# A convolution summed in PSUM, and a gate's tanh written where it is used

## The chip, the cores and the metric

The kernel runs on one core of one Trainium2 chip. The metric is the device time of one launch in microseconds, from runs on the chip: less is better. TensorE is called PE below, VectorE DVE, ScalarE ACT, GpSimd POOL, and SyncE, which only issues DMAs, SP.

## The reference

One inference step of a two-layer trunk: an RG-LRU layer (Hawk), then an HGRN2 layer, on 1024 prompt tokens and 8 sequences of 4 decode tokens, all in float32. The change concerns the first layer alone:

```python
xn = _rmsnorm(x, g_norm)
u = xn @ w_in                              # 1024 -> 2 * 1536
xb, gate = u[..., :W_LRU], u[..., W_LRU:]
xp = concatenate([buf, xb], axis=1)        # the causal convolution, 4 taps
xc = b + sum(w[k] * xp[:, k:k + T] for k in range(4))
xh = xc.reshape(Bsz, T, 16, 96)            # 16 blocks of 96 columns
r = sigmoid(einsum('btni,nij->btnj', xh, w_r) + b_r)
ig = sigmoid(einsum('btni,nij->btnj', xh, w_i) + b_i)
log_a = -8 * softplus(-lam) * r
a = exp(log_a)
bterm = sqrt(-expm1(2 * log_a)) * (ig * xc)
h = scan(a, bterm)                         # h[t] = a[t] * h[t-1] + bterm[t]
y = h * silu(gate)
x = x + y @ w_out
```

## The kernel before

All 1056 tokens lie along the free dimension in three chunks of 352 columns (the last chunk is 320 prompt columns and the 32 decode tokens); features lie on the 128 partitions. A product of two float32 matrices is made of three fp32r matmuls of rounded high and low parts (`mm3`, lines 290 to 292). Weights come in by DMA as `wraw`; ACT rounds them to the high part (`whi`, L436), and POOL or DVE subtracts to get the low part (`wlo`, L374).

PSUM has eight banks: four with the tag `mm`, taken in turn by the main products, and four with the tag `hg`, for the block-diagonal gate products and norms. A main product with 1024 inputs is 24 matmuls of 352 columns, an out product (`out`, a third of 1536 inputs) is 9.

The 1536 columns of the recurrent branch are worked on in four groups g = 0 to 3 of three 128-row tiles (j = 0 to 2). For each group there are gate products (`gate(g)`), conv products (`conv(g)`, nine of them: three tiles, three chunks), the recurrence (`lru(g)`) and the out products (`out(g)`). The main products follow each other in this order: the three chunks of gate(0) and conv(0), gate(1), conv(1), gate(2) with lru(1) beside it, conv(2), out(0) with lru(2) beside it, gate(3) for one tile, conv(3), out(1) with lru(3) beside it, the rest of gate(3), and the last out products (`out_last`).

*A conv product* ends in a `mm` bank `ps`. ACT copies it to `xb` (L578, in SBUF, with room for the three columns before it; in the first group DVE writes `xb` with the norm multiplied in), and the last three columns to the next `xb` (L581). In the third chunk POOL and ACT also build the windows of the decode tokens in `xb`, and every step is done once for 320 prompt and once for 32 decode columns. ACT writes tap 3 times its weight plus the bias to an SBUF row `t` (L591; `t` is one of three rows of the tile `k`). DVE adds the other three taps to `t` (L594), ACT rounds `t` to the high part in `Z` (L597), and DVE writes the low part (L598). The bank is free as soon as ACT has copied it out.

*The recurrence.* A group has 384 rows, which is four of the reference's blocks of 96. The fourth block is made of rows 32j to 32j + 31 of tile j; the other 96 rows of each tile are a block of their own. These are gathered by DMA into `fo` (six copies a chunk) and multiplied on their own. The tanh of the three plain blocks goes from an `hg` bank to `R` (L666, 128 rows). The fourth block's goes from its bank to `td`, a part of the tile `ST` (L672, 96 rows), and three DMAs copy its 32-row pieces into their places in `R`, over rows that L666 wrote. Then follow, for each tile, exp (L679) and tanh (L681) on ACT, the sum of the high and low part on POOL (L685, to one of two rows of `k`), DVE's L686, a square root on ACT (L689), two products on DVE (L690, L692), and the scan (L706) and the gate (L716).

*The order* on every engine is written out by a planner in the kernel, `Flow`. Each step is added with its engine, a cost in microseconds, the keys that it reads and writes (a bank or a row is a key), and a priority. `plan` lays all steps out in time, `back` gives them due times, and after some turns the best plan is emitted; each engine then runs its steps in exactly that order. For the first layer, a DMA is taken to land 2.6 us after its issue begins, and its bytes are added at 250 KB a microsecond. A DVE step with `both` is taken to wait for POOL's running step. The second layer has a plan of its own, which starts from the first one's end times.

Of the kernel before, what the change touches and what calls it, by code (L numbers as in the profile page):

```python
# [14 lines left out]
F32 = mybir.dt.float32  # L15
# [3 lines left out]
AF = mybir.ActivationFunctionType  # L19
ALU = mybir.AluOpType  # L20
# [30 lines left out]
CH = 352  # L51
# [9 lines left out]
class Flow:  # L61
# [67 lines left out]
    def plan(self, key, stop=None):  # L129

        n = len(self.ops)
        left = [len(o[3]) for o in self.ops]
        ready = list(self.born)
        wait = {e: [] for e in self.ENGINES}
        free = dict(self.busy)
        dma = locked = taken = 0.0
        for i in range(n):
            if not left[i]:
                wait[self.ops[i][0]].append(i)
        starts, ends, took, order = [0.0] * n, [0.0] * n, [0.0] * n, []  # L140
        for _ in range(n):
            t0, e = min((max(free[e], min(ready[i] for i in q)), e) for e, q in wait.items() if q)
            q = wait[e]
            i = min((j for j in q if ready[j] <= t0), key=lambda j: (key[j], j))
            q.remove(i)
            order.append(i)
            _, us, _, _, _, kb, _, both = self.ops[i]
            if both and not self.exact and free["POOL"] > t0:
                us = max(us, free["POOL"] - t0 + us - 0.13)
            elif both and self.exact:  # L150
                us += max(0.0, taken - t0 - 0.07)
                locked = t0 + us
            elif e == "POOL" and self.exact:
                us += max(0.0, locked - t0 - 0.035)
                taken = t0 + us
            starts[i] = t0
            free[e] = end = t0 + us
            if kb and self.exact:
                dma = max(dma + kb / 250.0, t0 + 2.4 + kb / 600.0)
                end = dma - 2.15 - kb / 250.0  # L160
            elif kb:
                dma = max(dma, t0 + 2.6) + kb / 250.0
                end = dma - 2.15 - kb / 250.0
            ends[i] = max(free[e], dma if kb else 0.0)
            took[i] = us
            if i == stop:
                break
            for j in self.after[i]:
                ready[j] = max(ready[j], free[e] if (i, j) in self.soft else end + self.lag(i, j))
                left[j] -= 1  # L170
                if not left[j]:
                    wait[self.ops[j][0]].append(j)
        last = max(t for t, o in zip(ends, self.ops) if self.until in (None, o[0]))
        return last, starts, ends, order, took
# [83 lines left out]
def tile_trunk(ctx: ExitStack, tc: tile.TileContext, xT, xN, prm, hc, w0, wg, wo0, w1, wo1, s_in,  # L258
               yT, h_out, c_out, sp_out, ss_out):
    nc = tc.nc  # L260
    V, S, G, T, Q = nc.vector, nc.scalar, nc.gpsimd, nc.tensor, nc.sync
# [16 lines left out]
    def pc(name, j, n=1):  # L278
        a = PRM[name][0] + j
        return P[:, a:a + n]  # L280
# [64 lines left out]
    with ExitStack() as l0:  # L345
# [16 lines left out]
        def act(n, emit, r, w, prio=5, more=0.0, chain=None):  # L362
            fl.add("ACT", (0.09 + 0.00088 * n if fl.exact else 0.25 + 0.0007 * n) + more, emit, r, w, prio, line=chain)
# [193 lines left out]
        def conv(g, head=False):  # L557

            items = []
            for j in range(3):  # L560
                m = 3 * g + j
                mine = {}

                def evac(c, ps, pk, by=None, j=j, m=m, mine=mine):
                    n = CH if c < 2 else 1024 - 2 * CH
                    if c == 0:
                        mine[0] = next(xbs)
                        pool(3, lambda xb=mine[0][0]: G.memset(xb[:, :3], 0.0), (), (mine[0][1],), 2)
                    elif head:
                        mine[c] = next(xbs)  # L570
                        pool(3, lambda xb=mine[c][0]: G.tensor_copy(xb[:, :3], tails[:, 4 * j:4 * j + 3]), (("tail", j),), (mine[c][1],), 0)
                    xb, xk = mine[c]
                    t, tk = next(ts)
                    if by:
                        dve(n, lambda: V.tensor_tensor(xb[:, 3:3 + n], ps[:, :n], by[0], op=ALU.mult), (pk, by[1]), (xk,), 0)
                        pool(3, lambda: G.tensor_copy(tails[:, 4 * j:4 * j + 3], xb[:, n:n + 3]), (xk,), (("tail", j),), 1)
                    else:
                        act(n, lambda: S.copy(xb[:, 3:3 + n], ps[:, :n]), (pk,), (xk,), 0)  # L578
                    if c < 2 and not by:
                        nx, nk = mine[c + 1] = (tails[:, 4 * j:], ("tail", j)) if head else next(xbs)  # L580
                        act(3, lambda: S.copy(nx[:, :3], ps[:, CH - 3:CH]), (pk,), (nk,), 0)  # L581
                    parts = [(xb[:, :3 + n], t[:, :n], lambda ap, i: ap[:, i:i + n], n)]
                    if c == 2:
                        xs = xb[:, 323:379].rearrange("p (b j) -> p b j", j=7)
                        pool(24, lambda: G.tensor_copy(xs[:, :, :3], cs[:, m]), (("hct",),), (xk,), 1)
                        act(32, lambda: S.copy(xs[:, :, 3:], ps[:, n:CH].rearrange("p (b j) -> p b j", j=4)), (pk,), (xk,), 0)
                        pool(3, lambda: G.tensor_copy(cst[:, m, 0, :], xb[:, 320:323]), (xk,), (("cst", m),), 4)
                        pool(24, lambda: G.tensor_copy(cst[:, m, 1:, :], xs[:, :, 4:7]), (xk,), (("cst", m, 1),), 4)
                        parts.append((xs, t[:, n:].rearrange("p (b j) -> p b j", j=4), lambda ap, i: ap[:, :, i:i + 4], 32))
                    for src, dst, sh, u in parts:  # L590
                        act(u, lambda src=src, dst=dst, sh=sh: S.activation(dst, sh(src, 3), AF.Identity, bias=pc("cb", m),  # L591
                                                                         scale=pc("cw", 36 + m)), (xk, ("P",)), (tk,), 1, 0.1)
                        for k in range(3):
                            dve(u, lambda src=src, dst=dst, sh=sh, k=k: V.scalar_tensor_tensor(  # L594
                                dst, sh(src, k), pc("cw", 12 * k + m), dst, op0=ALU.mult, op1=ALU.add), (xk, tk), (tk,), 1, True)
                    (a, ak), (b, bk) = xpart(j, 0, c), xpart(j, 1, c)
                    act(CH, lambda: S.copy(a, t), (tk,), (ak,), 1)  # L597
                    dve(CH, lambda: V.tensor_tensor(b, t, a.bitcast(F32), op=ALU.subtract), (tk, ak), (bk,), 1, True)  # L598

                items.append((w0[m], evac))  # L600
            return items

# [27 lines left out]
        def lru(g):  # L630
            for i, n in ((0, 4), (4, 2)):
                raw, rk = next(raws)
                u = 128 * n
# [13 lines left out]
            for c in range(NCH):  # L647
# [10 lines left out]
                for i, hb in ((0, hbr), (1, hbi)):  # L658
                    for j in range(3):
                        m = 3 * g + j  # L660
                        ps, pk = next(hg)
                        (a, ak), (b, bk) = xpart(j, 0, c), xpart(j, 1, c)
                        u = 3 * i + j
                        fl.add("PE", 0.48, lambda ps=ps, a=a, b=b, u=u: mm3(ps[:, :CH], (gh[:, u, :], gl[:, u, :]), a, b, True, True),
                               (ak, bk, ("gh", u // 4 * 4), ("gl", u // 4 * 4)), (pk,), 0)
                        act(CH, lambda ps=ps, R=R, i=i, j=j, hb=hb, m=m: S.activation(R[:, i, j], ps[:, :CH], AF.Tanh, bias=hb[:, m:m + 1],  # L666
                                                                           scale=0.5), (pk, ("sm",)), (("R", s, i, j),), 2, 0.05)
                    ps, pk = next(hg)

                    fl.add("PE", 0.48, lambda ps=ps, i=i: mm3(ps[:, :CH], (gsh[:, i, :], gsl[:, i, :]), fo[:, 0], fo[:, 1], True, True),  # L670
                           (("gs",), ("gsl",), ("fo",), *(("fo", n, j) for n in range(2) for j in range(3))), (pk,), 0)
                    act(CH, lambda ps=ps, i=i: S.activation(td[:, i], ps[:96, :CH], AF.Tanh, bias=hbd[:96, 4 * i + g:4 * i + g + 1],  # L672
                                                            scale=0.5), (pk, ("sm",)), [("ST", j, i) for j in range(3)], 2, 0.05)
                    for j in range(3):
                        w = slice(32 * j, 32 * j + 32)
                        dma(R[w, i, j], td[w, i], (("ST", j, i),), (("R", s, i, j),), 2, 45)
# [1363 lines left out]
```

## Time and profile before

| | |
|---|---|
| median of three runs | 1031.67 us (1030.27 to 1032.05) |
| the profiled execution | 1029.75 us |
| its span, first to last instruction | 1027.9 us |
| mean granted TensorE clock | 0.999 |
| busy: PE, DVE, ACT, POOL | 1013.2, 777.6, 610.3, 494.6 us |

The profile is of one execution. PE is its matmuls, PEld the weight loads that run beside them. A row of a group of instructions gives line, engine, operation, what is written and read (by the program's names, with shapes), how often, busy time, the mean in ns, and the idle time of that engine just before, with what ended it. "DVE R L686 <- DMA R<-ST" reads: DVE's instruction at line 686, which writes R, waited for the DMA that copies ST into R. Almost all DMAs of the first layer are issued from one line, L359, in SP's queue.

### The profile page before, as it was taken

How to read it: one execution, taken by the hardware profiler on the slowest of the kernel's cores; microseconds unless marked ns; L12 is line 12 of the kernel's file. 1: busy time of each engine (PE TensorE's matmuls, PEld its weight loads, DVE VectorE, ACT ScalarE, POOL GpSimd, SP SyncE). 2: the span in 40 equal slices, each digit the busy share in tenths (PEclk: the TensorE clock that was granted, in tenths of full speed). 3: DMA queues.
4: the chain of work that ended last, by engine and by line, in shares of the span. 5: the costliest groups of instructions: out<-in, count | busy, mean ns of one | idle time of the engine just before them, and what ended most of it. 6: DMA issues, size and time to landing. Idle time of an engine off the chain costs nothing.

```text
span 1027.9 us, 25651 instructions
## 1 busy us (share of the span) xinstructions
PE 1013.2 (99%) x9981; PEld 993.5 (97%) x9981; DVE 777.6 (76%) x1538; ACT 610.3 (59%) x1405; POOL 494.6 (48%) x579
## 2 busy tenths in 40 slices
PE   9999999999999999999999999999999999999997
PEld 9999999999999999999999999999999999999986
DVE  6899986798689688557798787787777777885537
ACT  7678656876765666434566474646565564752324
POOL 2435453454247254744235655564646464641544
PEclk9999999999999999999999999999999999999999
DMA  9611111214652478622113142423333333666204
GB/s 283 204 53 43 51 61 61 79 55 134 202 186 71 145 224 270 201 72 77 62 32 125 46 141 89 127 87 126 106 119 111 106 125 98 212 197 208 87 1 170
DMA packets 84442, 124.60 MB, mean 121 GB/s; under 512 B 11296, under 2 KB 61728, under 8 KB 84320
## 3 DMA queue, kind: packets, MB, share of 16 engines
q1 hardware_dynamic: 75104, 107.13, 33.6%
q10 hardware_dynamic: 9216, 15.84, 4.8%
q8 instruction: 78, 1.28, 0.5%
q14 instruction: 44, 0.36, 0.1%
HBM read 82.55 MB, written 33.87 MB: 113 GB/s over the span
## 4 chain that ended last, share of the span: by engine, by line
PE 86%; DVE 5%; ACT 3%; issue 2%; DMA 2%; POOL 1%; SPq 0%; POOLq 0%; DVEq 0%; ACTq 0%
PE mm L290 24%; PE mm L292 24%; PE mm L291 24%; PE hg L1281 2%; DVE k L594 2%; DMA R<-ST 1%; PE hg L1470 1%; PE hg L291 1%; PE hg L290 1%; PE hg L1513 1%; PE hg L292 1%; PE hg L1515 1%; PE hg L902 1%; PE hg L1538 1%; DVE R L706 1%
## 5 line engine op out<-in xcount | busy, mean ns | idle before, releaser
L290 PE MATMUL mm<-xh,whi 128*128 128x352 f32 (+1 forms) x1111 | 343.0, 309 | 0.3 <-DVE xo L737 0.3
L291 PE MATMUL mm<-xl,whi 128*128 128x352 f32 (+1 forms) x1111 | 340.8, 307 | 1.0 <-POOL xl L374 1.0
L292 PE MATMUL mm<-xh,wlo 128*128 128x352 f32 (+1 forms) x1111 | 341.5, 307 | 0.0
L374 POOL TENSOR_TENSOR wlo<-wraw,whi 128x256 fp32r<-128x256 f32 (+3 forms) x190 | 194.4, 1040 | 180.4 <-ACT whi L436 81.4
L291 PEld LDWEIGHTS mm<-xl,whi 128*128 128x128 f32 x1111 | 209.1, 188 | 1.5 <-POOL xl L374 1.2
L290 PEld LDWEIGHTS mm<-xh,whi 128*128 128x128 f32 x1111 | 208.8, 188 | 1.1 <-issue 0.6
L292 PEld LDWEIGHTS mm<-xh,wlo 128*128 128x128 f32 x1111 | 208.8, 188 | 0.2 <-DVE wlo L374 0.2
L290 PE MATMUL mm<-Z,whi 128*128 128x264 f32 (+1 forms) x507 | 152.2, 300 | 0.0
L291 PE MATMUL mm<-Z,whi 128*128 128x264 f32 (+1 forms) x507 | 150.5, 297 | 0.0
L292 PE MATMUL mm<-Z,wlo 128*128 128x264 f32 (+1 forms) x507 | 150.5, 297 | 0.0
L290 PEld LDWEIGHTS mm<-Z,whi 128*128 128x128 f32 x507 | 95.3, 188 | 2.7 <-ACT xh L1798 1.5
L594 DVE SCALAR_TENSOR_TENSOR k<-xb,prm_sb,k 128x352 f32<-128x352 f32 (+2 forms) x144 | 91.8, 646 | 7.4 <-ACT k L591 4.5
L291 PEld LDWEIGHTS mm<-Z,whi 128*128 128x128 f32 x507 | 95.5, 188 | 0.3
L292 PEld LDWEIGHTS mm<-Z,wlo 128*128 128x128 f32 x507 | 95.5, 188 | 0.2 <-POOL wlo L762 0.2
L374 POOL TENSOR_TENSOR wlo<-R,whi 128x256 fp32r<-128x256 f32 x74 | 59.4, 822 | 47.0 <-ACT whi L1640 40.6
L685 POOL TENSOR_TENSOR k<-Z 128x352 f32<-128x352 f32 x36 | 44.4, 1242 | 74.0 <-DVE R L686 64.4
L436 ACT CAST whi<-wraw 128x512 fp32r<-128x512 f32 (+2 forms) x75 | 41.2, 568 | 28.5 <-PE mm L291 11.6
L1710 DVE TENSOR_TENSOR k<-mm,k 128x264 f32<-128x264 f32 x58 | 24.5, 425 | 40.5 <-PE mm L292 33.7
L1640 ACT CAST whi<-wraw 128x512 fp32r<-128x512 f32 x61 | 37.6, 616 | 24.5 <-PE mm L291 24.4
L1707 ACT COPY k<-mm 128x264 f32<-128x264 f32 x84 | 31.7, 377 | 32.7 <-PE mm L292 29.8
L666 ACT ACTIVATE R<-hg,smalls 128x352 f32<-128x352 f32 x72 | 38.1, 550 | 14.7 <-DVE R L706 8.4
L290 PE MATMUL mm<-xh,Z 128*128 128x352 f32 x140 | 45.7, 327 | 0.0
(455 smaller groups left out, 2337.5 us busy)
## 6 DMA issues: line engine op xcount, KB each, us to landing
wraw<-in_w_dram SPq DMA_DIRECT2D x50, 256.0 KB, 3.3
wraw<-in_w_dram ACTq DMA_DIRECT2D x39, 256.0 KB, 3.2
wraw<-in_wo_dram SPq DMA_DIRECT2D x34, 192.0 KB, 2.7
R<-in_w_dram ACTq DMA_DIRECT2D x18, 256.0 KB, 2.8
si<-in_s_in_dram SPq DMA_DIRECT2D x8, 512.0 KB, 6.2
vt<-sg SPq DMA_DIRECT2D x8, 512.0 KB, 4.0
sg<-vt SPq DMA_DIRECT2D x32, 128.0 KB, 3.4
kt<-xo SPq DMA_DIRECT2D x8, 512.0 KB, 2.6
```

Source lines behind the costliest of these rows:

```text
L290: T.matmul(out, wh, xh, start=first, stop=False, skip_group_check=more)
L291: T.matmul(out, wh, xl, start=False, stop=False, skip_group_check=more)
L292: T.matmul(out, wl, xh, start=False, stop=last, skip_group_check=more)
L374: emit = lambda: e.tensor_tensor(b, x, a.bitcast(F32), op=ALU.subtract)
L436: act(m, lambda: S.copy(hi[:, :m], raw[:, :m]), rk, (hk,), prio, chain=chains[0])
L594: dve(u, lambda src=src, dst=dst, sh=sh, k=k: V.scalar_tensor_tensor(dst, sh(src, k), pc("cw", 12 * k + m), dst, op0=ALU.mult, op1=ALU.add ...
L666: act(CH, lambda ps=ps, R=R, i=i, j=j, hb=hb, m=m: S.activation(R[:, i, j], ps[:, :CH], AF.Tanh, bias=hb[:, m:m + 1], scale=0.5), (pk, ("s ...
L685: pool(CH, lambda x=x, a=a, b=b: G.tensor_tensor(x, a.bitcast(F32), b.bitcast(F32), op=ALU.add), (ak, bk), (xk,), 3)
L1281: T.matmul(ps[32 * j:32 * j + 32, n * w:n * w + w], B[:, o:o + 32], q(slice(o, o + 32)), start=True, stop=True, tile_position=(0, 32 * j))
L1640: act(512, lambda: S.copy(hi, raw), (rk,), (hk,), 2)
L1707: act(QT, lambda: S.copy(o[0], z[0]), (z[1],), (o[1],), 0)
L1710: dve(QT, lambda: V.tensor_tensor(o[0], z[0], u[0], op=ALU.add), (z[1], u[1]), (o[1],), 0)
```

## The change

There are three edits.

1. The convolution no longer has a row `t`. One ACT activation over all 352 columns writes tap 3 times its weight plus the bias back into the product's own PSUM bank (from the bank itself, or from `xb` in the first group), the other three taps are added there by DVE, and both parts are made from there. The first copy to `xb` stays. These steps get priority 0 in place of 1, and the DVE steps are no longer marked `both`.
2. In groups 2 and 3, the fourth block's tanh is done by three ACT instructions of 32 rows each, from the bank straight into the rows of `R`. `td` and the three DMAs are not used there. Groups 0 and 1 stay as they are.
3. The planner takes a DMA of the first layer that begins between 60 and 385 us to land 3.4 us after its issue begins, in place of 2.6.

```diff
             elif kb:
-                dma = max(dma, t0 + 2.6) + kb / 250.0
+                dma = max(dma, t0 + (3.4 if 60.0 < t0 < 385.0 else 2.6)) + kb / 250.0
...
                     xb, xk = mine[c]
-                    t, tk = next(ts)
...
-                    parts = [(xb[:, :3 + n], t[:, :n], lambda ap, i: ap[:, i:i + n], n)]
+                    parts = [(xb[:, :3 + n], ps[:, :n], lambda ap, i: ap[:, i:i + n], n)]
...
-                        parts.append((xs, t[:, n:].rearrange("p (b j) -> p b j", j=4), lambda ap, i: ap[:, :, i:i + 4], 32))
+                        parts.append((xs, ps[:, n:CH].rearrange("p (b j) -> p b j", j=4), lambda ap, i: ap[:, :, i:i + 4], 32))
+                    act(CH, lambda: S.activation(ps[:, :CH], xb[:, 3:3 + n] if by else ps[:, :CH], AF.Identity, bias=pc("cb", m), scale=pc("cw", 36 + m)),
+                        (xk, pk, ("P",)), (pk,), 0, 0.1)
                     for src, dst, sh, u in parts:
-                        act(u, lambda src=src, dst=dst, sh=sh: S.activation(dst, sh(src, 3), AF.Identity, bias=pc("cb", m),
-                                                                         scale=pc("cw", 36 + m)), (xk, ("P",)), (tk,), 1, 0.1)
                         for k in range(3):
                             dve(u, lambda src=src, dst=dst, sh=sh, k=k: V.scalar_tensor_tensor(
-                                dst, sh(src, k), pc("cw", 12 * k + m), dst, op0=ALU.mult, op1=ALU.add), (xk, tk), (tk,), 1, True)
+                                dst, sh(src, k), pc("cw", 12 * k + m), dst, op0=ALU.mult, op1=ALU.add), (xk, pk), (pk,), 0)
                     (a, ak), (b, bk) = xpart(j, 0, c), xpart(j, 1, c)
-                    act(CH, lambda: S.copy(a, t), (tk,), (ak,), 1)
-                    dve(CH, lambda: V.tensor_tensor(b, t, a.bitcast(F32), op=ALU.subtract), (tk, ak), (bk,), 1, True)
+                    act(CH, lambda: S.copy(a, ps[:, :CH]), (pk,), (ak,), 0)
+                    dve(CH, lambda: V.tensor_tensor(b, ps[:, :CH], a.bitcast(F32), op=ALU.subtract), (pk, ak), (bk,), 0)
...
+                    if g in (2, 3):
+                        for j in range(3):
+                            w = slice(32 * j, 32 * j + 32)
+                            act(CH, lambda ps=ps, R=R, w=w, i=i, j=j: S.activation(R[w, i, j], ps[w, :CH], AF.Tanh, bias=hbd[w, 4 * i + g:4 * i + g + 1],
+                                                                                   scale=0.5), (pk, ("sm",)), (("R", s, i, j),), 2, 0.05)
+                        continue
```

## The prediction

> **What bounds the kernel.** I read the page first, then busy time by stages, then the waits and the timeline of each engine around the few gaps of PE. TensorE works almost without a break.
>
> ```profile
> core 0: 1027.9 us, clock 0.999
> PE 1013.2 (99%) x9981; PEld 993.5 (97%) x9981; DVE 777.6 (76%) x1538; ACT 610.3 (59%) x1405; POOL 494.6 (48%) x579
> 210.00:255.00 45.00, 45.00 (x281) 45.00 (x281) 40.62 (x72) 31.55 (x69) 22.98 (x31) 1.00 0.35 103
> 255.00:307.00 52.00, 50.23 (x308) 49.16 (x307) 38.08 (x63) 38.90 (x64) 18.11 (x14) 1.00 0.63 193
> 307.00:351.00 44.00, 43.49 (x271) 43.20 (x270) 38.34 (x61) 24.47 (x61) 25.57 (x32) 1.00 0.32 94
> 351.00:397.00 46.00, 44.13 (x267) 42.61 (x266) 32.41 (x51) 36.80 (x60) 21.75 (x16) 1.00 0.75 228
> 600.00:700.00 100.00, 100.00 (x1441) 97.96 (x1440) 73.43 (x157) 57.69 (x147) 54.70 (x71) 1.00 0.37 114
> 700.00:800.00 100.00, 100.00 (x1557) 97.68 (x1556) 78.27 (x164) 59.50 (x162) 54.38 (x70) 1.00 0.35 112
> ```
>
> A stage row gives the stretch, its length, then busy time of PE, PEld, DVE, ACT and POOL. The change can only shorten the time where PE waits, and it touches the first layer alone. There PE is full up to 255 us (45.00 of 45). It has gaps in three stages: lru(2) beside out(0) (255 to 307), conv(3) (307 to 351), lru(3) beside out(1) (351 to 397). How much they hold depends on the reading. Idle PE is 1.77 + 0.51 + 1.87 = 4.15 us. Idle weight loads are 2.84 + 0.80 + 3.39 = 7.03. By counts, a matmul takes 45.00 / 281 = 0.160 us, so the stages have room for 325, 275 and 287 and ran 308, 271 and 267: 41 matmuls, 6.5 us. I take 6.5 as what can be won, 7.03 as the ceiling.
>
> The Trainium skill (Perfetto Trace Analysis, Identifying the Most-Contended Engine) says that matmul busy time is a poor measure of TensorE and that the busy share of weight loads is the one to use. By the PE column the ceiling would be 4.15 us, by that rule 7.03; the count, which needs neither, stands with the rule.
>
> **Where the gaps come from.** The timeline, start, duration, engine; in brackets the idle time and what ended it:
>
> ```profile
> 272.73 0.32 PE L292 MATMUL mm<-Z,wlo 128*128 128x352 f32 x1
> 274.25 0.40 PE L290 MATMUL hg<-fo,gsh 128*128 128x352 f32 x1 [1.20 <-DMA fo<-Z]
> 274.94 0.40 PE L291 MATMUL hg<-fo,gsh 128*128 128x352 f32 x1 [0.28 <-DMA fo<-Z]
> 338.36 0.32 PE L290 MATMUL hg<-Z,gh 128*128 128x352 f32 x1
> 339.19 0.43 PE L291 MATMUL hg<-Z,gh 128*128 128x352 f32 x1 [0.51 <-DVE Z L598]
> 368.47 0.32 PE L292 MATMUL mm<-Z,wlo 128*128 128x352 f32 x1
> 370.26 0.43 PE L290 MATMUL hg<-Z,gh 128*128 128x352 f32 x1 [1.47 <-ACT R L666]
> 363.33 1.79 SPq L359 DMA_DIRECT2D R<-ST  x3
> 367.08 0.69 ACT L679 ACTIVATE a<-R,smalls 128x352 f32<-128x352 f32 x1 [4.02 <-DMA R<-ST]
> 369.68 0.98 ACT L666 ACTIVATE R<-hg,smalls 128x352 f32<-128x352 f32 x2
> 264.65 0.53 DVE L686 SCALAR_TENSOR_TENSOR R<-R,k 128x352 f32<-128x352 f32 x1 [3.59 <-DMA R<-ST]
> 265.26 0.94 POOL L685 TENSOR_TENSOR k<-Z 128x352 f32<-128x352 f32 x1 [8.14 <-DVE R L686]
> 269.82 3.68 SPq L359 DMA_DIRECT2D fo<-Z  x6
> ```
>
> Read the last gap first. PE at 368.47 wants a hg bank and gets it at 370.26, 1.79 - 0.16 = 1.63 us late, when ACT's tanh (L666) has emptied it. That tanh was queued behind the exp at L679, which stood 4.02 us for the copy of the fourth block's tanh from ST into R. The gap at 272.73 is 1.52 + 0.69 - 0.32 = 1.89: the copies into fo left SP only from 269.82, in a stage where DVE's L686 waited 3.59 for an R copy and POOL stood 8.14 behind L686 with weight splits queued after it. The gap at 338.36, 0.83 - 0.16 = 0.67, is conv(3)'s own: DVE was late with L598.
>
> **The change part by part.** Rows for the prices (count, busy, mean ns, or min/median/max):
>
> ```profile
> L594 DVE SCALAR_TENSOR_TENSOR k<-xb,prm_sb,k 128x352 f32<-128x352 f32 (+2 forms) x144 | 91.8, 646 | 7.4 <-ACT k L591 4.5
> L594 DVE SCALAR_TENSOR_TENSOR k<-xb,prm_sb,k x144: 242/578/1611, 41.4 to 347.9; 128x352 f32<-128x352 f32 x72, 128x320 f32<-128x320 f32 x36, 128x32 f32<-128x32 f32 x36
> L553 DVE SCALAR_TENSOR_TENSOR sg<-sg,prm_sb,hg x15: 571/575/581, 444.9 to 494.6; 128x352 f32<-128x352 f32 x15
> L598 DVE TENSOR_TENSOR Z<-k,Z x36: 495/518/1618, 48.4 to 351.4; 128x352 fp32r<-128x352 f32 x36
> L598 DVE TENSOR_TENSOR Z<-k,Z 128x352 fp32r<-128x352 f32 x36 | 21.7, 604 | 6.0 <-ACT Z L597 6.0
> L737 DVE TENSOR_TENSOR xo<-mm,xo x18: 492/511/523, 244.6 to 385.0; 128x352 f32<-128x352 f32 x18
> L591 ACT ACTIVATE k<-xb,prm_sb 128x352 f32<-128x352 f32 (+2 forms) x48 | 28.8, 609 | 1.4 <-DVE Z L598 0.9
> L666 ACT ACTIVATE R<-hg,smalls 128x352 f32<-128x352 f32 x72 | 38.1, 550 | 14.7 <-DVE R L706 8.4 <-POOL ST L711 2.4 <-PE hg L292 2.0
> L672 ACT ACTIVATE ST<-hg,smalls 96x352 f32<-96x352 f32 x24 | 13.2, 548 | 1.0 <-PE hg L292 0.5 <-DMA R<-ST 0.3
> R<-ST SPq DMA_DIRECT2D x72, 44.0 KB, 2.0
> ```
>
> *Conv on DVE (C).* With two inputs from SBUF, these instructions reach 1611 and 1618 ns; with one from PSUM none passes 581. No row has DVE writing PSUM after a scalar_tensor_tensor, so the price is bounded: from below by 495 ns, the shortest L598 now, from above by no gain (646 and 604). I take the nearest rows, L553 (pointer, PSUM input): 72 x 575 + 36 x 542 (32 elements fewer, an estimate from 575) + 36 x 242 ns = 69.6 us against 144 x 646 = 93.0, and 36 x 511 against 36 x 604, 3.3 us less. DVE saves 26.7 us, 6.7 in each of four conv stages. DVE is no bound but in the 307 to 351 stage (38.34 of 44); of its gaps, at most 0.80, I take 0.6.
>
> The Trainium skill (VectorE: DVE Perf Modes, The TRN2 errata) charges a VectorE instruction 120 cycles at a PSUM source and 58 at SBUF, which speaks against this edit: 62 cycles at 0.96 GHz on 180 instructions, by estimate 11.6 us of the saving gone. Here L737 out of PSUM has a median of 511 ns and L598 out of SBUF 518, so the trace does not show that extra; by the page C would be about 0.3 us and the forecast 1029.0.
>
> *Conv on ACT.* 48 activations become 36. Between 441 (the plain PSUM copy's mean, below) and 609 ns, nearest L666, 550: some 20 us against 29.2. ACT has idle time in conv stages (24.47 of 44), so nothing of it is counted. Twelve fewer queue entries wait in front of nobody. The k ring is freed of conv; no gap is put down to it, so zero.
>
> *Fourth block's tanh, groups 2 and 3 (A and B).* For each of 3 chunks x 2 gates x 2 groups, one 96-row tanh becomes three 32-row ones, and three copies go: 36 DMAs off SP's queue (0.6 us each in it, 1.79 for three) and a round trip of 2.0 us at the median, up to 4 as above, off the way to exp and L686. ACT pays 24 x 0.548 = 13.2 us; 96 and 128 rows cost the same (548, 550), and I take that for 32 rows too, with zero as the other end. The hg bank is held 1.1 us longer, and SP's later copies into fo move up. What is late next is the bank itself: ACT in 351 to 397 goes from 36.80 to 36.80 + 12 x 0.548 = 43.4 of 46. Of the 3.39 us there I take A = 2.1 (the 1.63 and some small waits on L666); of the 2.84 in 255 to 307, B = 1.3, as the fo copies still need SP and 2 us.
>
> *Bank held through the convolution (E).* Now a mm bank is free after the ACT copies; then only after L598. Four banks serve all products, so product n's bank is wanted by n + 4. A 24-matmul product gives 3 x 3.84 us of grace, but behind conv(2) and conv(3) come out products of 9 matmuls, 1.44 us each:
>
> ```profile
> 242.74 0.32 PE L292 MATMUL mm<-xh,wlo 128*128 128x352 f32 x1
> 248.71 0.33 PE L290 MATMUL mm<-Z,whi 128*128 128x352 f32 x1
> 255.13 0.52 DVE L598 TENSOR_TENSOR Z<-k,Z 128x352 fp32r<-128x352 f32 x1
> 346.37 0.32 PE L290 MATMUL mm<-Z,whi 128*128 128x352 f32 x1
> 351.42 0.53 DVE L598 TENSOR_TENSOR Z<-k,Z 128x352 fp32r<-128x352 f32 x1 [2.43 <-ACT Z L597]
> 62.70 0.32 PE L290 MATMUL mm<-xh,whi 128*128 128x352 f32 x1
> 64.29 0.52 DVE L598 TENSOR_TENSOR Z<-k,Z 128x352 fp32r<-128x352 f32 x1
> L578 ACT COPY xb<-mm 128x352 f32<-128x352 f32 (+1 forms) x33 | 14.5, 441 | 21.2 <-PE mm L292 21.2
> ```
>
> conv(2)'s last product ends at 243.06 and its bank is wanted by the fourth out product at 248.71. Its shortest chain is copies 0.6, activation 0.55, six DVE steps 2.4, copy 0.44, subtract 0.51 and some 0.8 of hand-overs: 5.3 us, until 248.4. In today's order L598 ends at 255.65, 6.94 late. conv(3)'s last would be late by 351.95 - 346.37 = 5.58, and a bank in the first stage by 64.81 - 62.70 = 2.11. Together 14.6 us is the upper end, zero the lower (the order is made anew, with these waits in it). While PE stands at such a product, every later matmul, lru's too, stands behind it. I take 1.0, near the lower end, because 5.3 fits into 5.65 and DVE loses 6.7 us of work per stage.
>
> *DMA landing assumed 0.8 us later between 60 and 385 us.* It moves instructions and adds none. Up to 255 us PE is full and can only lose; the worst stage now loses 3.39; the gain's end is already in A and B. I take zero. Layer two is planned anew behind other end times: equal stretches there differ by 97.96 - 97.68 = 0.28 us per 100, so 1.1 either way over its 410 us, taken as zero.
>
> **Sum.** -2.1 - 1.3 - 0.6 + 1.0 = -3.0 us. The profiled execution took 1029.75 us (span 1027.9), 1.92 under the median 1031.67; moved alike, the median becomes 1028.7. About 0.2%, 2.1 us, is what a measurement can tell from no change.
>
> **Rivals.** *Slower:* DVE keeps lru(1)'s scans ahead of conv(2)'s last product, and PE stands 6.9 us at 248.71. Gains of 4.0 stay: 1034.6. It decides from a stand of 6.1 (4.0 + 2.1). For it: 0.3 us of slack and a DVE at 40.62 of 45; against: the new order knows the dependency and has lru's matmuls to put there. *No change:* ACT at 43.4 of 46 empties the hg banks no sooner than the DMA let it, so A is lost; B + C - E leave -0.9: 1030.8. For it the load; against, that 4.02 us of ACT's idle time there was this DMA. *All gaps go* and no bank is late: -7.03, 1024.6.
>
> **How the numbers follow.** Forecast 0.42, all gaps go 0.13, no change 0.25, slower 0.20. Hence faster 0.55, same 0.25, slower 0.20. The forecast's own range is 1026.5 to 1029.6. The range takes in the other cases, with layer two's 1.1 below: 1024.0 to 1034.6.
>
> **What would show it.** Right: no wait of ACT's L679 on R<-ST after 244 us; weight loads in 351 to 397 (that stage, wherever it lies) near 45 of 46; L594's maximum under 700 ns. E shows as PE waiting for DVE L598 at an out product's first matmul. Wrong, if PE waits for ACT tanh as long as now, or if the gaps only move to 400 to 520.

## The result, and the profile after

| | before | after |
|---|---|---|
| median of four runs | 1030.97 us (1030.16 to 1032.05) | 1023.10 us (1022.12 to 1023.38) |
| ratio, with its 95% interval | | 0.9921 (0.9904 to 0.9939) |
| the profiled execution | 1029.75 us | 1023.16 us |
| its span | 1027.9 us | 1021.4 us |

The change made the kernel faster by 7.9 us by the medians (three of the four runs before are those shown above), and by 6.6 us between the two profiled executions, 6.5 in span. The forecast was -3.0 us, 1028.7. The time lies below the range, whose lower end was 1024.0.

The page of the kernel after: busy time of the engines, and the shares of the chain of work that ended last.

```profile
PE 1011.6 (99%) x9981; PEld 993.9 (97%) x9981; DVE 759.2 (74%) x1538; ACT 619.3 (61%) x1417; POOL 475.6 (47%) x579
PE 94%; DMA 2%; DVE 2%; ACT 1%; POOL 1%; issue 0%; SPq 0%; POOLq 0%; ACTq 0%
```

The same line of the page before:

```profile
PE 86%; DVE 5%; ACT 3%; issue 2%; DMA 2%; POOL 1%; SPq 0%; POOLq 0%; DVEq 0%; ACTq 0%
```

PE's own time in the span hardly moves (1013.2 to 1011.6). What moved is the chain: what is not PE held 14% of it, now 6%.

Busy time by stages of the kernel after (columns as in the prediction):

```profile
0.00:60.00 60.00, 58.53 (x358) 57.07 (x359) 47.27 (x116) 42.57 (x97) 19.70 (x33) 1.00 0.67 211
210.00:255.00 45.00, 45.00 (x281) 44.81 (x280) 38.85 (x78) 35.05 (x76) 19.81 (x32) 1.00 0.33 95
255.00:307.00 52.00, 52.00 (x325) 52.00 (x324) 37.68 (x62) 45.16 (x76) 20.92 (x17) 1.00 0.64 198
307.00:351.00 44.00, 44.00 (x276) 44.00 (x275) 33.15 (x65) 28.15 (x65) 18.51 (x31) 1.00 0.25 74
351.00:397.00 46.00, 46.00 (x287) 46.00 (x286) 40.45 (x58) 40.87 (x68) 21.56 (x16) 1.00 0.80 257
```

and the first stage of the kernel before:

```profile
0.00:60.00 60.00, 58.95 (x362) 57.90 (x363) 46.36 (x114) 41.26 (x93) 19.05 (x31) 1.00 0.67 211
```

The three stages with gaps are full: idle weight loads there were 7.03 us and are 0.00. The first 60 us hold 2.93 of them against 2.10, so 0.83 more, and 210 to 255 us 0.19 more. That makes 7.03 - 0.83 - 0.19 = 6.0 us. The start of the last out products shows the same; their first matmul, from the timeline before and then after:

```profile
410.98 0.32 PE L290 MATMUL mm<-Z,gh 128*128 128x352 f32 x1
```

```profile
405.06 0.32 PE L290 MATMUL mm<-Z,gh 128*128 128x352 f32 x1
```

5.92 us of the 6.5 are won by there. From there to the end the span was 1027.9 - 410.98 = 616.9 and is 1021.4 - 405.06 = 616.3 us, which gives the other 0.6.

ACT's timeline after, around the fourth block's tanh in lru(3), beside the one of before in the prediction:

```profile
360.65 1.00 ACT L665 ACTIVATE R<-hg,smalls 128x352 f32<-128x352 f32 x2
361.54 1.67 ACT L674 ACTIVATE R<-hg,smalls 32x352 f32<-32x352 f32 x3
363.23 0.68 ACT L686 ACTIVATE R<-R,smalls 128x352 f32<-128x352 f32 x1
363.82 0.67 ACT L684 ACTIVATE a<-R,smalls 128x352 f32<-128x352 f32 x1
```

L674 is the new 32-row tanh, L684 the exp that was L679. Where ACT stood 4.02 us for the copy out of ST, it now spends 1.67 on three tanh and goes straight on. The waits from 244 to 400 us after, the largest that remain on these steps (total, times, longest):

```profile
ACT Z L596 <- DVE mm L593: 3.6, 5, 1.0
DVE R L691 <- ACT R L674: 3.2, 4, 1.0
```

The same rows before:

```profile
DVE R L686 <- DMA R<-ST: 15.1, 7, 3.9
ACT a L679 <- DMA R<-ST: 9.2, 5, 4.0
ACT Z L597 <- DVE k L594: 10.9, 8, 3.0
```

No engine waits for R<-ST any more there, and PE waits for nobody between 255 and 397 us.

### The profile page after: what moved, and what is told of

The parts are those of the page before. It is cut to its first block, busy times and chain, and to the rows that moved or that the text cites. A ratio compares the mean times of both kernels' runs of the same rounds, so it can differ in the third digit from the quotient of the medians.

```text
span 1021.4 us, 25581 instructions
## 1 busy us (share of the span) xinstructions
PE 1011.6 (99%) x9981; PEld 993.9 (97%) x9981; DVE 759.2 (74%) x1538; ACT 619.3 (61%) x1417; POOL 475.6 (47%) x579
## 4 chain that ended last, share of the span: by engine, by line
PE 94%; DMA 2%; DVE 2%; ACT 1%; POOL 1%; issue 0%; SPq 0%; POOLq 0%; ACTq 0%
PE mm L290 26%; PE mm L292 26%; PE mm L291 26%; PE hg L1286 2%; PE hg L292 2%; PE hg L291 2%; PE hg L290 2%; PE hg L1475 1%; PE hg L1518 1%; PE hg L1520 1%; DMA R<-in_xN_dram 1%; PE hg L1543 1%; DMA a<-in_w_dram 1%; PE hg L1495 0%; PE hg L1373 0%
## 5 line engine op out<-in xcount | busy, mean ns | idle before, releaser
L374 POOL TENSOR_TENSOR wlo<-wraw,whi 128x256 fp32r<-128x256 f32 (+3 forms) x190 | 189.1, 1011 | 223.0 <-ACT whi L436 118.1
L593 DVE SCALAR_TENSOR_TENSOR mm<-xb,prm_sb,mm 128x352 f32<-128x352 f32 (+2 forms) x138 | 67.5, 491 | 13.8 <-ACT mm L589 9.3
L290 PE MATMUL mm<-xh,Z 128*128 128x352 f32 x140 | 45.5, 325 | 0.0
L292 PE MATMUL mm<-xh,Z 128*128 128x352 f32 x140 | 45.2, 323 | 0.0
```

What stands on the lines that cost most here:

```text
L290: T.matmul(out, wh, xh, start=first, stop=False, skip_group_check=more)
L292: T.matmul(out, wl, xh, start=False, stop=last, skip_group_check=more)
L374: emit = lambda: e.tensor_tensor(b, x, a.bitcast(F32), op=ALU.subtract)
```

## The experiments

Each kernel was timed beside the kernel before on the same chip; medians of the kernel before were 1030.5 to 1031.1 us. "Idle loads" are the idle weight loads from 255 to 397 us, summed over the three stages (7.03 before, 0.00 after).

### One part at a time

**conv_only**: edit 1 alone; edits 2 and 3 are taken back. Here and below, a diff is against the kernel after unless the text says otherwise.

```diff
-                dma = max(dma, t0 + (3.4 if 60.0 < t0 < 385.0 else 2.6)) + kb / 250.0
+                dma = max(dma, t0 + 2.6) + kb / 250.0
...
-                    if g in (2, 3):
-                        for j in range(3):
...
-                        continue
```

> The first edit alone (convolution summed in its bank), against the kernel before. Round-trip theory (PE's gaps from 255 to 397 us come from engines that stand behind the fourth block's DMA copies): only the gap by DVE in conv(3) and some of the slack goes, 0.5 to 2 us faster, and ACT's exp still waits for the copies from ST for some 8 us in lru(3). DVE theory (DVE at over 85% in the conv stages delays everything behind it, the copies too): 4 us or more faster, and idle weight loads between 255 and 397 us fall from 7.0 to under 3. Bank theory (the held bank costs): PE waits for DVE or ACT of the convolution at the first out products, 1 to 7 us slower.

Measured: 1029.27 us, 0.9990 (0.9978 to 1.0002). Its stages:

```profile
255.00:307.00 52.00, 51.44 (x318) 50.79 (x317) 36.69 (x60) 36.73 (x60) 16.91 (x15) 1.00 0.70 211
307.00:351.00 44.00, 44.00 (x276) 44.00 (x275) 32.15 (x61) 28.59 (x66) 16.01 (x30) 1.00 0.27 77
351.00:397.00 46.00, 46.00 (x285) 45.57 (x284) 35.84 (x51) 31.98 (x52) 25.17 (x18) 1.00 0.76 235
400.00:440.00 40.00, 38.68 (x239) 37.71 (x238) 25.03 (x45) 17.64 (x40) 27.99 (x32) 1.00 0.67 205
```

Of the 7.03 us idle loads 1.64 are left, and the last out products start at 406.86, 4.1 us earlier; but the rest takes 1026.2 - 406.86 = 619.3 us, 2.4 longer. From 400 to 440 us 2.29 us of weight loads are idle. Its waits name one cause of it, weights' low parts from POOL:

```profile
PE mm L292 <- POOL wlo L761: 1.1, 2, 0.8
```

From 244 to 400 us the waits for the round trip are still there:

```profile
DVE R L685 <- DMA R<-ST: 13.8, 8, 4.3
ACT a L678 <- DMA R<-ST: 4.3, 4, 3.0
```

So the convolution alone closes most of the gaps with the round trip in place: DVE stands for the copies nearly as long as before (13.8 us against 15.1, by the rows above), ACT half as long (4.3 against 9.2). The idle loads came out as the DVE theory had them (under 3 us), the time as the round-trip theory had it. Most of what edit 1 wins is lost again behind 400 us: PE is there earlier, and part of what it needs is not.

**tanh_only**: edit 2 alone; the convolution's lines and the landing are those of before.

```diff
+                    t, tk = next(ts)
...
-                    parts = [(xb[:, :3 + n], ps[:, :n], lambda ap, i: ap[:, i:i + n], n)]
+                    parts = [(xb[:, :3 + n], t[:, :n], lambda ap, i: ap[:, i:i + n], n)]
...
-                dma = max(dma, t0 + (3.4 if 60.0 < t0 < 385.0 else 2.6)) + kb / 250.0
+                dma = max(dma, t0 + 2.6) + kb / 250.0
```

> The second edit alone (fourth block's tanh straight into R in groups 2 and 3), against the kernel before. Round-trip theory: 4 to 6 us faster, weight loads in the lru(3) stage near full, the 0.67 us gap in conv(3) stays. DVE theory: under 2 us faster, since DVE stays as late as now. ACT theory (13 us more on ACT hold the gate banks): no gain, PE waits for ACT's tanh instead of for a copy.

Measured: 1023.51 us, 0.9927 (0.9914 to 0.9940), nearly all of the gain.

```profile
255.00:307.00 52.00, 51.61 (x319) 51.13 (x318) 38.15 (x65) 47.27 (x80) 18.50 (x16) 1.00 0.61 189
307.00:351.00 44.00, 44.00 (x276) 44.00 (x275) 38.38 (x63) 27.50 (x64) 23.29 (x31) 1.00 0.37 109
351.00:397.00 46.00, 46.00 (x288) 46.00 (x287) 36.64 (x54) 41.92 (x70) 23.09 (x17) 1.00 0.77 236
```

Idle loads: 0.87. Conv(3)'s own gap, which was expected to stay, is gone too, with DVE as busy as before in that stage (38.38 against 38.34) and the convolution in its SBUF row. So the length of DVE's convolution steps was not enough to make it.

**land_only**: edit 3 alone, as a diff against the kernel before.

```diff
-                dma = max(dma, t0 + 2.6) + kb / 250.0
+                dma = max(dma, t0 + (3.4 if 60.0 < t0 < 385.0 else 2.6)) + kb / 250.0
```

> The third edit alone (a DMA taken to land 0.8 us later between 60 and 385 us; not one instruction more or less), against the kernel before. Order theory (a more careful order alone takes away the waits on copies): 2 us or more faster, with fewer waits of ACT and DVE on the copies from ST. Round-trip and DVE theories: within 1 us of before; a loss is as likely as a gain.

Measured: 1031.90 us, 1.0012 (1.0000 to 1.0024). Idle loads 4.84, but the last out products start later, at 412.78: the gaps moved forward (210 to 255 us now lacks 1.19). Conv(3)'s gap is gone here as well (44.00 of 44), by the order alone. The landing by itself wins nothing.

### Two parts together

**conv_tanh** (edits 1 and 2), **conv_land** (1 and 3), **tanh_land** (2 and 3): each is the kernel after with one edit taken back, by the lines shown above.

conv_tanh:

```diff
-                dma = max(dma, t0 + (3.4 if 60.0 < t0 < 385.0 else 2.6)) + kb / 250.0
+                dma = max(dma, t0 + 2.6) + kb / 250.0
```

conv_land:

```diff
-                    if g in (2, 3):
-                        for j in range(3):
...
-                        continue
```

tanh_land:

```diff
-                    parts = [(xb[:, :3 + n], ps[:, :n], lambda ap, i: ap[:, i:i + n], n)]
+                    parts = [(xb[:, :3 + n], t[:, :n], lambda ap, i: ap[:, i:i + n], n)]
```

> First and second edit without the third. If the third edit matters only as a part of the whole (it moves transfers ahead of a shorter chain), this is 1 to 3 us slower than all three together, some 5 to 7 us under before. If the third edit is nothing, 7 to 8 us under before, as all three. If the first and second overlap (either alone takes away the same gaps), their two single gains sum to more than this one.

> First and third edit, without the direct tanh. So far the convolution alone took 4.1 us of PE's gaps before the last out products away and gave 2.4 back behind them (ratio 0.999), the landing alone gained nothing (1.001). If the third edit is a help to the first, 2 us or more under before; if edits only add up, 0 to 1.5 us under before; the copies from ST are there, so exp still waits for them. The round-trip theory says that this cannot come near the 7 us of the direct tanh.

> Second and third edit, without the convolution in PSUM. The direct tanh alone made 0.993. Round-trip theory: the first edit has nothing left to gain, so this is level with all three, 0.991 to 0.994. If the convolution is worth something beside the tanh, this is 1 us or more slower than all three.

Measured: 1024.74, 0.9939 (0.9925 to 0.9953), idle loads 0.00; 1026.49, 0.9957 (0.9944 to 0.9969), idle loads 1.62; 1025.46, 0.9947 (0.9935 to 0.9960), idle loads 0.24. With the tanh the gaps of the three stages are all but gone whatever else is done; without it some stay. In tanh_land 1.25 us are lost from 210 to 255 us instead. No pair beats the tanh alone. In two of them the wait that the prediction called E stands in PE's timeline. In conv_land it stands at the third out product behind conv(2), one before the product for which it was worked out:

```profile
247.78 0.32 PE L292 MATMUL hg<-fo,gsl 128*128 128x352 f32 x1
249.51 0.43 PE L290 MATMUL mm<-Z,whi 128*128 128x352 f32 x1 [1.41 <-DVE Z L597]
```

and in conv_tanh, in the first group's products:

```profile
93.51 0.32 PE L292 MATMUL mm<-xh,wlo 128*128 128x352 f32 x1
94.45 0.43 PE L290 MATMUL mm<-xh,whi 128*128 128x352 f32 x1 [0.61 <-DVE Z L597]
```

L597 is the convolution's last reader of the bank (L598 before): 1.73 - 0.16 = 1.6 us and 0.94 - 0.16 = 0.8 us. In the kernel after the same out product stands so:

```profile
247.78 0.32 PE L292 MATMUL hg<-fo,gsl 128*128 128x352 f32 x1
248.00 0.43 PE L290 MATMUL mm<-Z,whi 128*128 128x352 f32 x1
```

0.06 us late. The wait is real, its size is a matter of the order, and in the order of the kernel after it is next to nothing.

### Round trip or queue

**tanh_sp**: tanh_only, and 36 DMAs of nearly the same size are put back into SP's queue, where the copies out of ST had been. They copy rows of a small tile to a spare array in DRAM that nobody reads. The diff is against tanh_only.

```diff
+    dmy = nc.dram_tensor("dmy", (36 * 32, ML * NB * 3), F32, kind="Internal").ap()
...
-                        dma(fo[w, i].bitcast(F32), x[w].bitcast(F32), (xk,), (("fo", i, j),), 1, 45)
+                        dma(fo[w, i].bitcast(F32), x[w].bitcast(F32), (xk,), (("fo", i, j),), 1, 45, chain="dmy" if g in (2, 3) else None)
...
+                        for j in range(3):
+                            n = 18 * (g - 2) + 6 * c + 3 * i + j
+                            dma(dmy[32 * n:32 * n + 32, :], hct[32 * j:32 * j + 32, :], (("hct",),), (("dmy", n),), 2, 45, chain="dmy")
```

> The direct tanh alone, with 36 more DMAs in SP's queue, of 32 x 288 from a row that nobody waits for to scratch memory, issued behind the fo copies of groups 2 and 3: the queue's load of the removed copies without their round trip. Round trip: the gain stays, within 1 us of the direct tanh alone (0.993). Queue load (the gain was SP's queue of 22 us made free, so that fo and the out rows move up): most of the gain goes, 0.997 or more, and PE waits for fo<-Z as before.

Measured: 1024.48 us, 0.9936 (0.9923 to 0.9948), idle loads 0.00. The DMAs by what they move, and two of its stages:

```profile
dmy<-hct SPq DMA_DIRECT2D x36, 36.0 KB, 1.6
```

```profile
255.00:307.00 52.00, 52.00 (x325) 52.00 (x325) 39.56 (x65) 46.48 (x78) 19.15 (x16) 1.00 0.64 201
351.00:397.00 46.00, 46.00 (x288) 46.00 (x287) 37.38 (x56) 41.15 (x71) 24.26 (x18) 1.00 0.74 233
```

SP's load is back and no gap is: the 36 issues did not cost the time. What is left is the round trip, behind which exp and L686 stood. The added copies differ from the ones out of ST in one more thing, as they wait for nobody, while a copy out of ST can stand at the head of SP's queue until ACT has written. In the kernel before, this does not account for the two gaps whose rows the prediction shows: from 255 to 275 us, around the first, SP waited for ACT 0.4 us, and from 351 to 371, around the other, not at all.

**tanh_g2** and **tanh_g3**: edit 2 alone, in one group each; and **tanh_all**: the kernel after with the direct tanh in all four.

```diff
-                    if g in (2, 3):
+                    if g == 2:                 # tanh_g2
+                    if g == 3:                 # tanh_g3
+                    if g in (0, 1, 2, 3):      # tanh_all
```

> The direct tanh alone, in group 2 only, against the kernel before. Round-trip theory: the gaps of lru(2), 2.7 us in out(0), go, those of lru(3), 3.2 us in out(1), stay with ACT's waits on the copies there: 2 to 3.5 us faster. If lru(2)'s delay is what makes lru(3) late, nearly the whole 7 us.

> The direct tanh alone, in group 3 only. Round-trip theory: out(1)'s 3.2 us go, out(0)'s 2.7 stay: 2.5 to 4 us faster. The two halves should sum to the 7 us of both; if they sum to much more, either takes away the same gaps.

> All three edits, with the direct tanh in all four groups. Round-trip theory: PE had no gap beside lru(0) and lru(1), so nothing is left to take there: within 1 us of all three edits (0.992). ACT theory: 13 us more on ACT from 57 to 245 us, where the first stages have ACT at 55 of 70: 1 us or more slower than all three. Queue theory: SP is freed earlier, some 1 us faster.

Measured: 1026.28, 0.9960 (0.9948 to 0.9971); 1026.57, 0.9964 (0.9952 to 0.9976); 1026.14, 0.9952 (0.9939 to 0.9966). Group 2's tanh belongs to lru(2) (255 to 307 us), group 3's to lru(3). The two stages of tanh_g2:

```profile
255.00:307.00 52.00, 52.00 (x325) 52.00 (x324) 37.81 (x65) 46.76 (x79) 20.24 (x16) 1.00 0.61 188
351.00:397.00 46.00, 45.24 (x279) 44.74 (x279) 34.02 (x56) 36.27 (x62) 21.31 (x15) 1.00 0.78 242
```

and of tanh_g3:

```profile
255.00:307.00 52.00, 50.04 (x301) 49.76 (x300) 36.91 (x61) 38.29 (x62) 19.51 (x15) 0.97 0.65 199
351.00:397.00 46.00, 46.00 (x288) 46.00 (x287) 36.00 (x57) 41.41 (x70) 20.45 (x15) 1.00 0.82 253
```

The stage with the direct tanh is full. The other keeps 1.26 of 3.39 us, or 2.24 of 2.84. So the two groups are not quite separate: group 2's tanh also took 2.1 us out of lru(3)'s stage. And what is left in tanh_g3 is put down to something else than the round trip. PE's one stand there is for DVE, which waited for rows of the input from DRAM:

```profile
264.70 0.53 DVE L743 TENSOR_TENSOR k<-mm,k 128x352 f32<-128x352 f32 x1 [5.14 <-DMA k<-in_xT_dram]
265.28 0.43 PE L290 MATMUL mm<-Z,whi 128*128 128x352 f32 x1 [1.96 <-DVE k L743]
```

(L743 is the L737 of before. In this stretch the granted clock was 0.97, and 301 matmuls took 50.04 us; at 0.160 us each they would have taken 48.2. So the idle time does not hold all that was lost.) For lru(2)'s stage it is therefore shown that the direct tanh empties the gap, but not that every gap that can open there is the round trip's. The two gains, 4.3 and 4.0 us, come to 8.3 against 7.2 for both at once, so they nearly add.

In groups 0 and 1 PE had no gap to close, and tanh_all has a ratio of 0.9952 where the kernel after had 0.9921. That is 3.0 us slower: the ACT theory had 1 us or more, the round-trip theory at most 1. It lacks 1.23 us of weight loads from 60 to 210 us and 1.49 from 210 to 255, and PE's waits name the convolution's bank; whether ACT's added work is behind that is not shown:

```profile
PE mm L290 <- DVE Z L597: 2.1, 2, 1.2
```


### What of the convolution

**conv_flags**: edit 1's marks alone (priority 0, no `both`), as a diff against the kernel before; the sum stays in SBUF.

```diff
-                                                                         scale=pc("cw", 36 + m)), (xk, ("P",)), (tk,), 1, 0.1)
+                                                                         scale=pc("cw", 36 + m)), (xk, ("P",)), (tk,), 0, 0.1)
-                                dst, sh(src, k), pc("cw", 12 * k + m), dst, op0=ALU.mult, op1=ALU.add), (xk, tk), (tk,), 1, True)
+                                dst, sh(src, k), pc("cw", 12 * k + m), dst, op0=ALU.mult, op1=ALU.add), (xk, tk), (tk,), 0)
```

(and so for L597 and L598)

**conv_oldmarks**: conv_only with the old marks (priority 1, `both`), as a diff against conv_only.

```diff
-                                dst, sh(src, k), pc("cw", 12 * k + m), dst, op0=ALU.mult, op1=ALU.add), (xk, pk), (pk,), 0)
+                                dst, sh(src, k), pc("cw", 12 * k + m), dst, op0=ALU.mult, op1=ALU.add), (xk, pk), (pk,), 1, True)
```

**conv13**: the kernel after, but the first group's convolution keeps its SBUF row.

```diff
+                    t, tk = next(ts) if head else (ps[:, :CH], pk)
...
```

(and, for the first group alone, the steps and marks of before)

> The kernel before, convolution still in the SBUF row, with only the planner's marks of the first edit: priority 0, and no wait for POOL assumed for its DVE steps. Order theory: the marks alone make the order that took PE's gaps in out(0) and out(1) from 5.9 to 1.5 us with the convolution in PSUM: same here, 2 us or more faster before the last out products. DVE theory (those gaps went because the sums no longer stretch beside POOL): no gain, within 1.5 us of before, L594 still reaching 1.6 us.

> The first edit alone (sums in the bank), with the planner's old marks: priority 1, and its DVE steps laid out as if they waited for POOL. DVE theory: shorter steps help under any order, so PE's gaps in out(0) and out(1) are under 3 us, level with the first edit alone (0.999) or better. Order theory: without the new marks the bank is held too long and PE waits for the convolution's DVE steps, 1 us or more slower than before.

> All three edits, but the first group's convolution stays in its SBUF row. If the bank held through the convolution costs in the first 95 us (PE's losses up to the third chunk's products went from 2.8 to 3.4 us, and to 5.4 without the third edit), this is 0.5 to 1 us under all three edits, 0.991. If that is the search over the first 60 us and not the bank, level with all three, 0.992 to 0.993.

Measured: 1036.46, 1.0056 (1.0042 to 1.0071), idle loads 8.58; 1027.22, 0.9970 (0.9958 to 0.9981), idle loads 1.29; 1024.92, 0.9945 (0.9932 to 0.9958), idle loads 0.00. The marks alone cost 5.9 us, which neither theory had; with the sum in PSUM, too, the new marks are 2.0 us slower than the old ones (1029.27 and 1027.22), which is no more than another order can make (below). The SBUF steps stretch there as they did before (min, median, max in ns):

```profile
L594 DVE SCALAR_TENSOR_TENSOR k<-xb,prm_sb,k x144: 232/577/1560, 41.8 to 353.3; 128x352 f32<-128x352 f32 x72, 128x320 f32<-128x320 f32 x36, 128x32 f32<-128x32 f32 x36
```

The idle loads that edit 1 empties go with the sum in PSUM: with either marks 1.3 to 1.6 us are left. Whether DVE's shorter steps do it, or the fewer ACT steps or the freed rows of `k`, no run tells apart. That the first group's banks are held longer costs nothing that can be seen, since taking that away (conv13) brought no gain: it is 1.8 us slower than the kernel after, which neither expectation had.

### How much is the order

**before_seed2**, **after_seed2**, **tanh_only_seed2**: three kernels with another seed in the planner's search, so another order of the same instructions.

```diff
-        rng = Random(1)
+        rng = Random(2)
```

> The kernel before with another seed of the planner's search over the first 60 us: no step changes, only the order found. If a re-laid order is worth little, within 0.5 us of before; if orders scatter as the combinations do, up to 2 us either way.

> All three edits with another seed. If their 0.992 is the edits, 0.991 to 0.993; if it was a lucky order, 0.993 to 0.996 like the other combinations with the direct tanh. PE's gaps in out(0) and out(1) should stay away in both cases.

> The direct tanh alone with another seed. If orders scatter little, 0.992 to 0.994 as before; by the scatter between combinations, 0.992 to 0.996. If this and the other seed's run of all three edits change places, the first and third edit are worth nothing that can be told beside the tanh.

Measured: 1031.51, 1.0008 (0.9998 to 1.0019), idle loads 6.27; 1023.92, 0.9939 (0.9923 to 0.9955), idle loads 0.00; 1024.19, 0.9940 (0.9925 to 0.9956), idle loads 0.06. The gaps of the kernel before are there in the other order too, and the direct tanh empties them in both. The whole change and the tanh alone lie 0.0006 apart with one seed and 0.0001 with the other, while one kernel moves by up to 0.0018 between the seeds. So what edits 1 and 3 add beside edit 2 cannot be told from the scatter of the orders. tanh_land, conv13 and tanh_all lie 0.0024 to 0.0031 above the kernel after, somewhat more than that scatter, but each is known in one order only. No kernel was faster than the kernel after.

## Why the prediction was wrong

**Direction and place: right.** PE bounds the kernel, what was won lay in PE's gaps from 255 to 397 us (but for 0.6 us behind 405), and taking the DMA round trip from in front of exp and L686 empties them, in two orders. The round trip is not the whole condition: with the convolution in PSUM most of the gaps go although it stays (conv_only). The ceiling of 7.03 us from idle weight loads was the right one: by 405 us the kernel after has won all of it but the 1.0 us that it lost earlier. The PE column, 4.15, would have been too small. The Trainium skill (Perfetto Trace Analysis, Identifying the Most-Contended Engine) prefers weight loads as the measure of TensorE, and the traces bear it out.

**The sizes of A and B: the step that failed.** Of A's 3.39 us 2.1 were taken, because "what is late next is the bank itself", with ACT at an expected 43.4 of 46. Of B's 2.84 1.3 were taken, "as the fo copies still need SP and 2 us". Both went whole (tanh_sp: 46.00 of 46.00 and 52.00 of 52.00). Neither reserve had a row in which something was in fact late behind the round trip. ACT stands at 40.87 of 46, not at 43.4: the 32-row tanh were priced rightly, but the stretch holds another piece of the order than before. Nor would 43.4 have made the bank late. In tanh_all ACT is that busy, and no weight load is idle:

```profile
351.00:397.00 46.00, 46.00 (x287) 46.00 (x287) 34.79 (x61) 43.34 (x73) 20.45 (x16) 1.00 0.80 249
```

The copies into fo are still there, and PE does not wait for them. That is 2.8 us of the miss.

**C: right in size, wrong in cause.** 0.6 was taken of 0.80, and all went; but tanh_only and land_only emptied that gap as well, with the convolution unchanged. Edit 1 alone took 5.4 us of the gaps, far more than C. So C and A, B are not separate terms: either edit empties most of the same gaps, and the sum of what they win alone (1.4 + 7.2 us) is more than the 5.9 of conv_tanh. Even the 1.4 is one order's value: without the tanh, edit 1 has 0.9990, 0.9970 and 0.9957 (conv_only, conv_oldmarks, conv_land). The prices were near: L593 in PSUM costs 71.0 us against 69.6 by the prediction, of which the page's row for the `mm` banks is

```profile
L593 DVE SCALAR_TENSOR_TENSOR mm<-xb,prm_sb,mm 128x352 f32<-128x352 f32 (+2 forms) x138 | 67.5, 491 | 13.8 <-ACT mm L589 9.3
```

and the first group's six in `hg` banks come to 3.5 more (6 x 0.582, below).

**E: too high.** 1.0 us was taken; the kernel after shows 0.06 at the third out product and 0.19 in all of 210 to 255 us. It was not unfounded: conv_land pays 1.6 us at the third out product. The reason that was given does not hold, though. The chain of conv(2)'s last product took not 5.3 us but 6.5 in the kernel after, from the end of its matmuls at 242.78 to the end of its L597 at 249.25, which is more than the 5.65 that were there. (The 0.8 of hand-overs in the 5.3 stood on no row; here the one from ACT's L589, done at 244.81, to DVE's L593 at 244.84 is 0.03. What made the chain long is the other work of ACT and DVE between its steps.) It cost nothing at the fourth out product, because the new order has 18 gate matmuls of lru ahead of it where the old one had 9, and it begins at 250.04 with no idle time before it:

```profile
248.73 0.52 DVE L597 TENSOR_TENSOR Z<-mm,Z 128x352 fp32r<-128x352 f32 x1
250.04 0.32 PE L290 MATMUL mm<-Z,whi 128*128 128x352 f32 x1
```

So E was a choice among the planner's orders, and one value could not be had from the profile of before. That the kernel after loses 1.02 us before 255 us, close to E, is chance: 0.83 of it lies in the first 60 us, and conv13, which does not hold the first group's banks, loses 3.38 there against 2.93.

**Zero for the landing:** right for the edit alone (land_only, 1.0012). Beside others it moved the ratio either way: -0.0033 (conv_land against conv_only), +0.0020 (tanh_land against tanh_only), -0.0018 (the kernel after against conv_tanh). **Layer two:** 0.6 us won, within the 1.1 allowed either way.

**The sum again.** With the measured sizes: -7.03 in the three stages, +0.83 in the first 60 us, +0.19 in 210 to 255, -0.6 behind 405 us: -6.6, as the profiled executions have it. That is 3.6 us of the miss of 5.6. The other 2.0 lie between the profiled execution and the median: before, it was 1.92 under its median, and the prediction let that distance stand; after, it lies 0.06 above its own. That part is the spread of executions, no mechanism: runs of the kernel before lie between 1027.5 and 1034.2.

**The rivals.** "All gaps go" had a chance of 0.13 and is what happened. Its time, 1024.6, less the 1.1 us of layer two would put the lower end of the range at 1023.5, not 1024.0; the 1023.10 lies below both. "No change", in which ACT takes the DMA's place, fell with the rows of L674 and L684 and with tanh_all's stage above. "Slower" needed a stand of 6.1 us at the fourth out product; the kernel after has none there, and 0.06 at the third, where conv_land has 1.6.

## What to carry to other kernels

Where an in-order queue stands behind a small DMA round trip and the bottleneck's gaps follow from that queue, take the whole of the gaps as the first estimate of the gain unless a row shows the next thing that is late; a reserve for a wait that no row shows is a guess. Here the whole went. Two edits that act on one gap are not two terms of a sum. Where an order is planned anew, compare a part with the whole under a second seed before crediting the part with a few tenths of a per cent.

## What was not expected of the hardware

Durations of the convolution's steps after (min, median, max in ns; L597 is the subtraction, L589 the activation, L674 the 32-row tanh):

```profile
L593 DVE SCALAR_TENSOR_TENSOR mm<-xb,prm_sb,mm x138: 248/556/590, 38.7 to 344.5; 128x352 f32<-128x352 f32 x66, 128x320 f32<-128x320 f32 x36, 128x32 f32<-128x32 f32 x36
L593 DVE SCALAR_TENSOR_TENSOR hg<-xb,prm_sb,hg x6: 576/582/590, 37.3 to 46.7; 128x352 f32<-128x352 f32 x6
L597 DVE TENSOR_TENSOR Z<-mm,Z x34: 499/517/525, 43.7 to 345.8; 128x352 fp32r<-128x352 f32 x34
L589 ACT ACTIVATE mm<-mm,prm_sb x33: 601/617/645, 50.0 to 341.5; 128x352 f32<-128x352 f32 x33
L674 ACT ACTIVATE R<-hg,smalls x36: 528/546/550, 248.4 to 381.9; 32x352 f32<-32x352 f32 x36
```

A DVE step that reads and writes a PSUM bank in place costs about what one in SBUF costs at its median (556 and 582 against 578; the 556 and 578 mix widths, and at 352 columns alone they are 590 and 585). It did not stretch: the longest took 590 ns, where the SBUF form reached 1611. The Trainium skill (SBUF — State Buffer, SBUF: two separate sides) states that a DVE instruction with two SBUF inputs can be locked out by GpSimd for the whole of an instruction. The traces agree with that. Before, 31 of the 144 L594 and 4 of the 36 L598 took over 700 ns, and POOL was at work for over 0.1 us beside every one of them; after, POOL was at work as long beside 75 of the 144 L593, and none took over 590. One such pair before:

```profile
231.31 1.16 POOL L685 TENSOR_TENSOR k<-Z 128x352 f32<-128x352 f32 x1 [0.96 <-DVE Z L598]
231.59 1.26 DVE L598 TENSOR_TENSOR Z<-k,Z 128x352 fp32r<-128x352 f32 x1
```

The extra that the Trainium skill (VectorE: DVE Perf Modes, The TRN2 errata) charges for a PSUM source is again not seen: 517 ns out of PSUM, 518 out of SBUF before.

ACT's activation in place in PSUM took 617 ns, above the 550 that were taken from L666 and above the upper bound of 609, which was a mean over shorter forms too. A tanh of 32 rows takes as long as one of 96 or 128 (546 against 548 and 550), as was assumed.
